# Latent attention taken in two groups of 256 queries, with the first pair's projection and routing in the second group's stream

## The chip, the cores and the metric

The kernel runs on one core of a Trainium2 chip. The metric is the device time of one execution in microseconds; the median over executions is compared. TensorE is PE, VectorE is DVE, ScalarE is ACT, GpSimd is POOL, and SP issues most of the loads.

## What is computed

A backbone of two layers over 512 latent tokens and 256 context tokens, width 1024, all in float32. Layer 0 mixes with a state-space scan, layer 1 with latent attention of 8 heads. Each layer ends in an expert retrieval: a query per head picks 16 of 16384 experts, so every token has 128 experts with gates. Of layer 1 only the latent tokens are needed. The parts that the change touches:

```python
def mla_attend(q_nope, q_rope, k_nope, k_rope, v):
    scale = (MLA_NOPE + MLA_ROPE) ** -0.5
    s = (jnp.einsum('bqhd,bkhd->bhqk', q_nope, k_nope)
         + jnp.einsum('bqhr,bkr->bhqk', q_rope, k_rope))
    p = jax.nn.softmax(s.astype(jnp.float32) * scale, axis=-1).astype(v.dtype)
    return jnp.einsum('bhqk,bkhd->bqhd', p, v)
...
    o_l, o_c = mla_mixer(...)
    h_lat = layer_norm(ALPHA * h_lat + mod_l[2] * o_l, ln_g[i, 0], ln_b[i, 0])
    f_l = peer_channel(h_lat * (1.0 + mod_l[4]) + mod_l[3], peer_w_q[i], peer_keys[i], peer_u[i], peer_v[i])
...
    idx, gate = peer_route(t, w_q, keys)
        act = jax.nn.gelu(jnp.einsum('td,tkd->tk', hb, u_tab[ib]), approximate=False) * gb
        return jnp.einsum('tk,tkd->td', act, v_tab[ib])
```

## The kernel before

Tokens come in tiles of 128: 0 and 1 are context, 2 to 5 latent. In layer 1, tile 5 is *gathered* (its experts' rows of `peer_u` and `peer_v` are fetched one by one by POOL and reduced on DVE), and tiles 4, 2 and 3 are *dense*: PE multiplies them with all 128 blocks of 128 experts, and a matrix of gates, mostly zero, picks from the result.

`mla` first projects down to the latents `cqT` and `ckvT` and makes the values `v`. Then for each of 8 heads `project` makes the head's queries (`qps`, rotary `rp` and `rs` for two heads at once) and keys (`kp_mla`, all 768 tokens), each split into a high and a low part by ACT and DVE. `scores` takes 128 queries at a time (four steps of a head): five matmuls for each of two score tiles `sp_mla`, maximum, exponential, scaling. `values`, two steps later, transposes the weights (`tp_ps`) and, at the head's last step, multiplies with `v` (`op_mla`).

After attention `out_steps` multiplies with the output weights (`op`), and its `norm` makes the normalised rows `h`; `query_steps` transposes and modulates them (`mt_ps`, `mT`), splits them into `Hall` (the dense experts' operand), and makes routing queries (`qp`). Both take a pair of tiles: the first pair is (5, 4), the second (2, 3). Before, both pairs' steps stand in one list, woven by `E1` and `E2`. `route` then finds a tile's experts, nearly all on DVE (lines 946 to 1021: `top16` and one-hots `oh`). `gate_matrix` turns a dense tile's routing into gate matrices, 16 groups of 8 tokens a tile (`e` and `o`, then `g_ps`, then `stage` to memory). `ahead` takes 48 of the 128 blocks of the dense product with U early (`U` split into `Uh`, `Ul`; `s_ps`), and `gather` yields gathered rows. `dense_held` does the rest: `s_ps` for the other 80 blocks and `acc` for all.

`merge` interleaves such streams: each step yields a time, and the stream with the smallest sum goes next; `side` streams don't keep the loop alive. This writes the program order. A scheduler then sets each engine's queue, and each engine takes its queue in that order. Tiles come from pools with a fixed number of buffers (20 of 4 KB per partition, 8 of 2 KB, 5 of `row`, 8 banks of PSUM); an instruction that writes a tile waits until the buffer is free. A use of a gathered row keeps its place in the program order on DVE. `peer_memory` closes the memory of attention's weights and opens `Hall` in it.

Of the kernel before, what the change touches and what calls it, by code (L numbers as in the profile page):

```python
# [20 lines left out]
D = 1024  # L21
# [24 lines left out]
KU, LH, KL, GQ = 2, 4, 2, 4  # L46
GA = 3
# [60 lines left out]
class Net:  # L108
# [763 lines left out]
    def peer_setup(self, l, dense, gather):  # L872
        self.keysT = self.t4([128, 8, 128], "keysT")
        self.load(self.keysT, self.a["peer_keysT"][l])
        self.tiles, self.gathered = dense, gather
        self.h1 = {}
        self.qT, self.m, self.gat, self.routed = {}, {}, {}, {}
        self.gm = self.dram.tile([16, 128, len(dense), 4, 8, 32], F32, name=f"gm{l}")
# [6 lines left out]
    def query_steps(self, l, pair, H):  # L885
# [504 lines left out]
    def mla(self, dense, gather):  # L1390
# [76 lines left out]
        wukv = W[:, 6144:10240].rearrange("p (k n) -> p k n", k=2)  # L1467
        cosT, sinT = W[:, 10240:10752], W[:, 10752:11264]
# [3 lines left out]
        for k in range(2):  # L1472
            self.load(wukv[:, k, :], a["mla_w_ukv"][k * 128:(k + 1) * 128, :])
# [3 lines left out]
        wv = wukv.rearrange("p k (h x d) -> p k h x d", h=8, x=2)  # L1477
        for ti in range(6):
            for hf in range(2):
                vp = self.ps([128, 4, 128], "vp")  # L1480
                for k in range(2):
                    PE.matmul(out=vp, lhsT=ckvT[k][:, ti * 128:(ti + 1) * 128], rhs=wv[:, k, hf * 4:(hf + 1) * 4, 1, :],
                              start=(k == 0), stop=(k == 1))
                S.copy(out=v[ti][:, hf * 512:(hf + 1) * 512].rearrange("p (h d) -> p h d", h=4), in_=vp)
        oT, heads = [], {}

        def project(h):
            if h % 2 == 0:
                oT.append(self.t4([128, 2, T_LAT], "oT"))
                rp, rs = self.ps([128, 512], "rp"), self.ps([128, 512], "rs")  # L1490
                for k in range(3):
                    PE.matmul(out=rp, lhsT=wuq[:, k, 1024 + h * 64:1024 + (h + 2) * 64], rhs=cqT[k], start=(k == 0), stop=(k == 2))
                for k in range(3):
                    PE.matmul(out=rs, lhsT=wuqs[:, k, h * 64:(h + 2) * 64], rhs=cqT[k], start=(k == 0), stop=(k == 2))
                qr, qt = self.t2([128, T_LAT], "qr"), self.t2([128, T_LAT], "qt")
                V.tensor_tensor(out=qr, in0=rp, in1=cosT, op=ALU.mult)
                V.tensor_tensor(out=qt, in0=rs, in1=sinT, op=ALU.mult)
# [169 lines left out]
```

## Time and profile before

| | |
|---|---|
| median of 2 executions | 4099.25 us (4098.07 to 4100.43) |
| profiled execution | 4107.66 us |
| its span in the trace | 4105.9 us |
| PE, DVE, ACT, POOL busy | 91%, 75%, 35%, 30% of the span |
| attention of layer 1 | 2466 to 2687 us |
| output and query projections | 2687 to 2788 us |
| four routes | 2788 to 2990 us |
| gate matrices, then the dense stage | 2990 to 3207 us, 3207 to 4090 us |

The profile is of one execution, and its stretches add up to its own time, which is 8.4 us above the median. The rows give for each engine how long it was busy in a stretch, for an instruction its start and duration, and in brackets how long its engine sat idle before it and what ended that. The limits of the stretches are the starts of the first instruction of the next kind of work.

### The profile page before, as it was taken

What the parts mean: (1) busy time and instruction counts of PE and PEld (TensorE: products, weight loads), DVE (VectorE), ACT (ScalarE), POOL (GpSimd) and SP (SyncE); (2) the same over time, 40 slices, a digit from 0 to 9 for tenths busy, and PEclk for the clock granted to TensorE, in tenths of its full rate; (3) what the DMA queues carried; (4) which work ended last, traced back from release to release, by engine and by line L of the source; (5) the groups of instructions that cost most, each with busy time, mean ns of one, the idle gap of its engine ahead of it and who ended that gap; (6) DMA issues with size and microseconds to landing.
All of it is one profiled execution on the core that took longest, in us unless ns stands there. A gap on an engine that the chain in (4) does not pass through costs nothing.

```text
span 4105.9 us, 52738 instructions
## 1 busy us (share of the span) xinstructions
PE 3719.0 (91%) x18955; PEld 3031.4 (74%) x18955; DVE 3068.7 (75%) x6143; ACT 1450.2 (35%) x2527; POOL 1238.6 (30%) x940
## 2 busy tenths in 40 slices
PE   6759999888689999999999989998887899999998
PEld 3537768677667878778888855568887788888887
DVE  9784387976867788888898844438977677777764
ACT  1321123366632232232332243323466333333332
POOL 5743000022412455556555300000011344444410
PEclk7879999899999999999999999999999999999999
DMA  5457234377888899999999820144477889888873
GB/s 182 134 176 247 80 131 152 96 241 249 293 311 290 291 338 352 337 354 330 342 338 346 301 98 3 44 169 140 123 234 247 317 327 334 318 320 321 328 271 102
DMA packets 380007, 986.06 MB, mean 240 GB/s; under 512 B 64992, under 2 KB 145376, under 8 KB 375136
## 3 DMA queue, kind: packets, MB, share of 16 engines
q1 hardware_dynamic: 198688, 501.34, 35.4%
q0 software_dynamic: 110592, 402.70, 27.4%
q10 hardware_dynamic: 70464, 78.65, 5.5%
q8 instruction: 149, 2.44, 0.2%
q14 instruction: 114, 0.93, 0.1%
HBM read 892.28 MB, written 90.21 MB: 239 GB/s over the span
## 4 chain that ended last, share of the span: by engine, by line
PE 57%; DVE 14%; issue 12%; DMA 7%; POOL 6%; ACT 3%; SPq 0%; POOLq 0%; ACTq 0%; DVEq 0%
PE s_ps L1111 20%; PE acc L1180 8%; PE acc L1255 8%; POOL row L1323 5%; PE qp L920 3%; PE op L791 3%; DMA U<-in_peer_uT 3%; DMA row<-in_peer_v,idx 2%; PE g_ps L1076 2%; PE zp L762 2%; DVE Ul L306 1%; PE op_mla L1560 1%; DVE w L645 1%; PE yp L697 1%; DMA row<-in_peer_u,idx 1%
## 5 line engine op out<-in xcount | busy, mean ns | idle before, releaser
L1111 PE MATMUL s_ps<-Hs,Uh 128*128 128x512 f32 (+1 forms) x4096 | 1187.4, 371 | 13.5 <-ACT Uh L305 13.5
L1323 POOL DMA_INDIRECT row<-in_peer_u,idx x384 | 528.8, 1377 | 2025.2 <-DVE row L1330 1148.2
L1111 PEld LDWEIGHTS s_ps<-Hs,Uh 128*128 128x128 f32 x4096 | 763.1, 190 | 116.2 <-ACT Uh L305 18.7
L1111 PE MATMUL s_ps<-Hs,Ul 128*128 128x512 f32 (+1 forms) x2048 | 759.6, 371 | 27.2 <-DVE Ul L306 27.1
L1255 PE MATMUL acc<-Ws,A 128*128 128x512 f32 x2976 | 689.1, 393 | 37.5 <-ACT A L305 21.4
L1255 PEld LDWEIGHTS acc<-Ws,A 128*128 128x128 f32 x2976 | 564.3, 190 | 160.6 <-ACT A L305 21.9
L1323 POOL DMA_INDIRECT row<-in_peer_v,idx x384 | 502.9, 1310 | 516.8 <-DVE f L1335 460.7
L306 DVE TENSOR_TENSOR Ul<-U,Uh 128x1024 fp32r<-128x1024 f32 x256 | 312.0, 1219 | 281.8 <-ACT Uh L305 273.6
L1335 DVE SCALAR_TENSOR_TENSOR f<-row,act,f 128x1024 f32<-128x1024 f32 x381 | 487.1, 1278 | 33.8 <-DMA row<-in_peer_v,idx 32.2
L1330 DVE SCALAR_TENSOR_TENSOR row<-row,m 128x1024 f32<-128x1024 f32 x384 | 461.0, 1218 | 42.7 <-DMA row<-in_peer_u,idx 41.7
L1111 PEld LDWEIGHTS s_ps<-Hs,Ul 128*128 128x128 f32 x2048 | 389.5, 190 | 82.3 <-DVE Ul L306 35.3
L305 ACT CAST Uh<-U 128x1024 fp32r<-128x1024 f32 x256 | 268.0, 1050 | 500.0 <-DMA U<-in_peer_uT 454.4
L1180 PE MATMUL acc<-Wh,A 128*128 128x512 f32 x1536 | 426.6, 391 | 12.2 <-ACT A L305 12.2
L1076 PE MATMUL g_ps<-o,o 128*128 128x128 f32 x1792 | 240.3, 293 | 114.5 <-ACT o L1059 72.1
L1180 PEld LDWEIGHTS acc<-Wh,A 128*128 128x128 f32 x1536 | 288.3, 188 | 66.7 <-ACT A L305 12.6
L1114 ACT ACTIVATE ge<-s_ps 128x512 f32<-128x512 f32 (+1 forms) x256 | 138.8, 543 | 556.4 <-PE s_ps L1111 551.1
L1076 PEld LDWEIGHTS g_ps<-o,o 128*128 128x128 f32 x1792 | 229.7, 206 | 126.2 <-ACT o L1059 124.5
L305 ACT CAST A<-ge 128x512 fp32r<-128x512 f32 (+1 forms) x256 | 144.6, 565 | 309.0 <-DVE ge L1236 227.1
L305 ACT CAST Ws<-W 128x512 fp32r<-128x512 f32 x256 | 152.1, 619 | 264.3 <-DMA W<-in_peer_v 217.7
L1180 PE MATMUL acc<-Wl,A 128*128 128x512 f32 x768 | 237.5, 390 | 0.0
L306 DVE TENSOR_TENSOR Ws<-W,Ws 128x512 fp32r<-128x512 f32 x256 | 174.3, 684 | 56.0 <-ACT Ws L305 55.7
L306 DVE TENSOR_TENSOR A<-ge,A 128x512 fp32r<-128x512 f32 (+1 forms) x256 | 158.5, 620 | 54.2 <-ACT A L305 53.7
(340 smaller groups left out, 4780.3 us busy)
## 6 DMA issues: line engine op xcount, KB each, us to landing
U<-in_peer_uT SPq DMA_DIRECT2D x256, 512.0 KB
W<-in_peer_v SPq DMA_DIRECT2D x256, 256.0 KB
W<-in_peer_v SPq DMA_DIRECT2D x128, 512.0 KB
gm<-stage ACTq DMA_DIRECT2D x28, 2048.0 KB
ada_wt<-in_ada_w SPq DMA_DIRECT2D x96, 512.0 KB
Gt<-gm SPq DMA_DIRECT2D x16, 2048.0 KB
Gt<-gm SPq DMA_DIRECT2D x16, 1536.0 KB
wq<-in_peer_w_q SPq DMA_DIRECT2D x40, 512.0 KB
```

Source lines behind the costliest of these rows:

```text
L305: self.nc.scalar.copy(out=hi, in_=x)
L306: lo_eng.tensor_tensor(out=lo, in0=x, in1=hi.bitcast(F32), op=ALU.subtract)
L791: nc.tensor.matmul(out=op, lhsT=y(i, k), rhs=W, start=(k == 0), stop=(k == KD - 1))
L920: PE.matmul(out=st["p"][:, h % 2, i * 128:(i + 1) * 128], lhsT=W[:, k, :], rhs=st[i][:, k, :], start=(k == 0), stop=(k == KD - 1))
L1076: PE.matmul(out=gp[:, t, :], lhsT=o[1][:, t4 * 4 + t, :], rhs=o[0][:, t4 * 4 + t, :], start=True, stop=True)
L1111: PE.matmul(out=sp, lhsT=x[:, k, :], rhs=self.Hs[:, y, k, :], start=(n == 0), stop=(n == 3 * KD - 1))
L1114: S.activation(out=ge, in_=sp, func=AF.Gelu)
L1180: PE.matmul(out=acc[d][hf], lhsT=A[b][:, x, c], rhs=Ws[y][:, hf * 512:(hf + 1) * 512], start=(b == 0 and n == 0), stop=(b == NB - 1 and n ...
L1255: PE.matmul(out=acc[hf][d], lhsT=A[b][:, x, c], rhs=Ws[:, y], start=(j == 0 and n == 0), stop=(j == SB - 1 and n == 2))
L1323: GP.indirect_dma_start(out=r, out_offset=None, in_=tab, in_offset=bass.IndirectOffsetOnAxis(ap=ik[:, k:k + 1], axis=0), element_offset=l ...
L1330: x = V.scalar_tensor_tensor(out=r, in0=r, scalar=1.0, in1=m, op0=ALU.mult, op1=ALU.mult, accum_out=act[:, k:k + 1])
L1335: x = V.scalar_tensor_tensor(out=f, in0=r, scalar=act[:, k:k + 1], in1=f, op0=ALU.mult, op1=ALU.add)
```

## The change

Attention runs over two groups of 256 queries, (tiles 4 and 5) and then (2 and 3), each over all heads; `project` is called for a pair and a head, one head ahead, and makes the keys of the head anew for each group. Keys and queries of a head stand in `kq`, half of a two-head buffer; the weights for values are loaded apart. While the second group is attended, the first pair's output projection, normalisation, queries and two routes stand in a side stream, and so does the gather. Only afterwards is `Hall` opened; the first pair's split into it is held back till then (`late`). The second pair's projection follows alone, beside the early blocks of U (which need all four tiles' queries), the gates (now begun when two tiles' queries are there) and the gather.

```diff
+TQ = 7.0
...
+    def query_steps(self, l, pair, H, late=False):
...
             if ti in self.tiles:
-                c = slice(i * 128, (i + 1) * 128)
-                H_ = H()
-                self.split(H_[:, 0, :, c], H_[:, 1, :, c], mT, nc.vector)
+                def parts():
+                    c = slice(i * 128, (i + 1) * 128)
+                    H_ = H()
+                    self.split(H_[:, 0, :, c], H_[:, 1, :, c], mT, nc.vector)
+
+                if late:
+                    self.late.append(parts)
+                else:
+                    parts()
...
-        W = self.big([128, 12288], "mla_w")
+        W = self.big([128, 9216], "mla_w")
...
+        wv = [self.t4([128, 8, 128], "wv") for _ in range(2)]
+        for k in range(2):
+            src = a["mla_w_ukv"][k * 128:(k + 1) * 128, :].rearrange("p (h x d) -> p h x d", h=8, x=2)
+            self.load(wv[k], src[:, :, 1, :])
+            self.load(wk[:, k], src[:, :, 0, :])
...
+        oT, heads = {}, {}
+
+        kq, pTs = self.t16([128, 2, 2 * T + 512], "kq", F32R), self.t16([128, 2, 6, 256], "pT")
+
+        def project(pair, h):
+
+            q0 = (min(pair) - 2) * 128
+            tq = slice(q0, q0 + 256)
+            if h % 4 == 0:
+                oT.setdefault(pair, []).append(self.t4([128, 4, 256], "oT"))
...
+                rp = self.ps([128, 2, 256], "rp")
+                for x, w in ((0, wuq[:, :, 1024 + h * 64:1024 + (h + 2) * 64]), (1, wuqs[:, :, h * 64:(h + 2) * 64])):
+                    for k in range(3):
+                        PE.matmul(out=rp[:, x], lhsT=w[:, k], rhs=cqT[k][:, tq], start=(k == 0), stop=(k == 2))
...
+            qnT = kq[:, h % 2, 2 * T:].rearrange("p (x q) -> p x q", x=2)
...
+                PE.matmul(out=qps, lhsT=wuq[:, k, h * 128:(h + 1) * 128], rhs=cqT[k][:, tq], start=(k == 0), stop=(k == 2))
...
+                    PE.matmul(out=kp[:, 0:n], lhsT=wk[:, k, h, :], rhs=ckvT[k][:, c0:c0 + n], start=(k == 0), stop=(k == 1))
+                self.split(kn[:, 0, c0:c0 + n], kn[:, 1, c0:c0 + n], kp[:, 0:n], V)
+            heads[pair, h] = qnT, qs, kn, pTs[:, h % 2]
...
+        def scores(pair, h, qi):
+
+            if h == qi == 0:
+                project(pair, 0)
+            qnT, qr, kn, _ = heads[pair, h]
...
+            if qi == 0 and h < 7:
+                project(pair, h + 1)
             return pe
 
-        def values(h, qi, pe):
-            pT = heads[h][3]
+        def values(pair, h, qi, pe):
+            pT = heads[pair, h][3]
             self.transpose_to(pT[:, :, qi * 128:(qi + 1) * 128], pe, 6)
-            if qi == 3:
-                op = self.ps([128, 512], "op_mla")
+            if qi:
+                op = self.ps([128, 256], "op_mla")
                 for k in range(6):
                     PE.matmul(out=op, lhsT=v[k][:, h * 128:(h + 1) * 128], rhs=pT[:, k, :], start=(k == 0), stop=(k == 5))
-                V.tensor_copy(out=oT[h // 2][:, h % 2, :], in_=op)
-            return 8.0
-
-        drain(pipeline([(lambda h=h, qi=qi: scores(h, qi), lambda pe, h=h, qi=qi: values(h, qi, pe))
-                        for h in range(8) for qi in range(4)], 2))
+                V.tensor_copy(out=oT[pair][h // 4][:, h % 4, :], in_=op)
+            return TQ
+
+        def attend(pair):
+            return pipeline([(lambda h=h, qi=qi: scores(pair, h, qi), lambda pe, h=h, qi=qi: values(pair, h, qi, pe))
+                             for h in range(8) for qi in range(2)], 2)
+
+        def rows(tile):
+            return [self.row_bc(self.mods, 14 * D, "m2", tile=tile), self.row_bc(a["ln_g"], 2 * D, "lng", tile=tile),
+                    self.row_bc(a["ln_b"], 2 * D, "lnb", tile=tile)]
+
+        def out(pair):
+            def y(i, k):
+                c = (pair[i] - min(pair)) * 128
+                return oT[pair][k // 4][:, k % 4, c:c + 128]
+
+            return self.out_steps(1, pair, a["mla_w_o"], y, lambda ti: self.hd[ti], lambda: self.rows2)
+
+        order = gather + dense
+        p, q = tuple(order[:2]), tuple(order[2:])
+        drain(attend(p))
         self.peer_setup(1, dense, gather)
-        self.peer_memory(1)
-        r = [self.row_bc(self.mods, 14 * D, "m2", tile=self.spare), self.row_bc(a["ln_g"], 2 * D, "lng", tile=self.spare),
-             self.row_bc(a["ln_b"], 2 * D, "lnb", tile=self.spare)]
-        order = gather + dense
-
-        def out(pair):
-            return self.out_steps(1, pair, a["mla_w_o"],
-                                  lambda i, k: oT[k // 2][:, k % 2, (pair[i] - 2) * 128:(pair[i] - 1) * 128], 
-                                  lambda ti: self.hd[ti], lambda: r)
-
-        p, q = tuple(order[:2]), tuple(order[2:])
-        (m0, q0), (m1, q1) = (self.query_steps(1, p, lambda: self.Hall[:, :, :, 0:256]),
+        self.rows2 = rows(lambda shape, name: self.pool.tile(shape, F32, tag="rows", bufs=3, name=name))
+        (m0, q0), (m1, q1) = (self.query_steps(1, p, lambda: self.Hall[:, :, :, 0:256], late=True),
                               self.query_steps(1, q, lambda: self.Hall[:, :, :, 256:512]))
-        o1 = out(q)
-        steps = out(p) + o1[:E1] + m0 + o1[E1:] + q0[:E2] + m1 + q0[E2:] + q1
-
         self.gathering = self.gather(1, R1)
+        first = chain(pipeline(out(p) + m0 + q0, LT), *(self.route(ti) for ti in p))
+        merge(attend(q), side=(first, self.gathering))
+        while len(self.qT) < 2:
+            next(first)
+
+        def memory(_):
+            self.peer_memory(1)
+            for f in self.late:
+                f()
+            self.rows2 = rows(self.spare)
+            return 0.0
+
+        steps = [(lambda: None, memory)] + out(q) + m1 + q1
         self.aheads = self.ahead(1, [b for b in range(128) if b % 8 < A1], 4)
-        self.gates = self.gate_matrices(4)
-        merge(scaled(pipeline(steps, LT), FA), chain(*(self.route(ti) for ti in order)), side=(self.aheads, scaled(self.gates, FG1)))
+        self.gates = self.gate_matrices(2)
+        merge(scaled(pipeline(steps, LT), FA), chain(first, *(self.route(ti) for ti in q)),
+              side=(self.aheads, scaled(self.gates, FG1), self.gathering))
```

What the scheduler made of it is seen at three places. The first is on PE, where the first pair's output projection (`op`) ends and the normalised rows are transposed (`mt_ps`). Before:

```order
L1560 MATMUL op_mla<-pT,v 128x512 x6
L791 MATMUL op<-wo,oT 128x512 x52
L296 MATMUL mt_ps<-ident,h 128x128 x8
L791 MATMUL op<-wo,oT 128x512
L904 MATMUL m_ps<-ident,mT 128x128 x4
L791 MATMUL op<-wo,oT 128x512
L904 MATMUL m_ps<-ident,mT 128x128 x4
L296 MATMUL mt_ps<-ident,h 128x128 x8
```

and in the changed kernel, where `sp_mla` are scores of the second group:

```order
L1531 MATMUL kp_mla<-ckvT,mla_w 128x512 x2
L1531 MATMUL kp_mla<-ckvT,mla_w 128x256 x2
L287 MATMUL tp_ps<-ident,pe 128x128 x6
L792 MATMUL op<-wo,oT 128x512 x10
L297 MATMUL mt_ps<-ident,h 128x128 x8
L912 MATMUL m_ps<-ident,mT 128x128 x5
L1548 MATMUL sp_mla<-kq 128x512
```

The 32 matmuls of the first pair were followed by 20 of the second pair; now the transposes stand right behind the last of the 32, and the next scores behind them.

The second place is on DVE, in attention. `mx`, `nm`, `rsm` and `pe` are a step's maximum, its negative, its reciprocal sum and its weights. Before:

```order
L1542 TENSOR_TENSOR nm<-mx 128x1
L1543 TENSOR_SCALAR nm<-nm 128x1
L1539 TENSOR_REDUCE mx<-sp_mla 128x1
L1549 TENSOR_TENSOR rsm<-smx 128x1
L1539 TENSOR_REDUCE mx<-sp_mla 128x1
L1550 RECIPROCAL rsm<-rsm 128x1
L1542 TENSOR_TENSOR nm<-mx 128x1
L1551 TENSOR_SCALAR pe<-pe,rsm 128x768
L1543 TENSOR_SCALAR nm<-nm 128x1
L1549 TENSOR_TENSOR rsm<-smx 128x1
L1550 RECIPROCAL rsm<-rsm 128x1
```

and in the last third of the second group now, where `rw`, `scr` and `tk_tmp` are routing's and `row` a gathered expert:

```order
L1556 TENSOR_TENSOR nm<-mx 128x1
L954 MAX rw_20778<-scr 128x8
L1557 TENSOR_SCALAR nm<-nm 128x1
L954 MAX rw_20778<-scr 128x8
L955 MAX_INDEX rw_20778<-rw_20778,scr 128x8
L1338 SCALAR_TENSOR_TENSOR row,act<-row,m 128x1024
L956 MATCH_REPLACE tk_tmp<-rw_20778,scr 128x128 x2
L957 MAX rw_20778<-tk_tmp 128x8 x2
L958 MAX_INDEX rw_20778<-rw_20778,tk_tmp 128x8 x2
L1563 TENSOR_TENSOR rsm<-smx 128x1
```

Routing's instructions and gathered rows stand between the links of one softmax. Of both routes only the second tile's one-hots come behind the last of attention.

The third place is on DVE where the gates (`e`, `o`) end. `Ul` is an early block's low part. Before, ahead of the dense stage's first `Wl`:

```order
L1330 SCALAR_TENSOR_TENSOR row,act<-row,m 128x1024
L1054 TENSOR_TENSOR e<-iota_68,iT 128x2048
L1062 TENSOR_TENSOR o_24260<-e,gT 128x768
L1330 SCALAR_TENSOR_TENSOR row,act<-row,m 128x1024 x3
L306 TENSOR_TENSOR Ul<-U,Uh 128x1024
L1330 SCALAR_TENSOR_TENSOR row,act<-row,m 128x1024 x4
L306 TENSOR_TENSOR Wl<-W,Wh 128x1024
```

and now, where the last two rows go on in turn for 13 blocks (`row` sometimes more than once):

```order
L1070 TENSOR_TENSOR o_24194<-e,gT 128x768
L1062 TENSOR_TENSOR e<-iota_68,iT 128x2048
L1070 TENSOR_TENSOR o_24215<-e,gT 128x768
L1338 SCALAR_TENSOR_TENSOR row,act<-row,m 128x1024
L307 TENSOR_TENSOR Ul<-U,Uh 128x1024
```

Fewer early blocks stand among the gates, and 13 remain behind them, where before 3 did on PE. Before the dense stage 90 gathered rows are used, 32 before the change.

## Rows read from the trace of the kernel before

**Rows 1.** The page, totals: busy us (share of the span) and instructions.
```profile
PE 3719.0 (91%) x18955; PEld 3031.4 (74%) x18955; DVE 3068.7 (75%) x6143; ACT 1450.2 (35%) x2527; POOL 1238.6 (30%) x940
```

**Rows 2.** Busy time in stretches of the second layer: us, then each engine (instructions).
```profile
core 0: us, PE busy (x) PEld busy (x) DVE busy (x) ACT busy (x) POOL busy (x), PEclk, DMA share, GB/s
2466.00:2687.00 221.00, 212.46 (x771) 119.89 (x770) 102.51 (x276) 84.61 (x227) 0.00 (x0) 0.98 0.10 36
2687.00:2788.00 101.00, 100.98 (x553) 69.64 (x551) 41.10 (x124) 24.96 (x57) 0.00 (x0) 1.00 0.49 162
2788.00:2990.00 202.00, 171.78 (x1053) 163.72 (x1053) 191.75 (x876) 87.48 (x136) 4.70 (x5) 0.93 0.42 134
2990.00:3184.00 194.00, 159.71 (x1070) 157.44 (x1071) 137.64 (x154) 132.04 (x239) 37.48 (x28) 0.94 0.74 246
...
3207.00:4090.00 883.00, 868.58 (x4224) 769.82 (x4224) 645.37 (x812) 304.14 (x421) 312.76 (x219) 1.00 0.82 295
```

**Rows 3.** PE in order of time, one head of attention: start, us, line, operation.
```profile
2556.90 5.42 PE L1560 MATMUL op_mla<-pT,v 128*128 128x512 f32 x12 [0.46 <-ACT pT L287]
...
2565.21 0.48 PE L1534 MATMUL sp_mla<-knT,qnT 128*128 128x512 f32 x1
...
2567.72 0.87 PE L286 MATMUL tp_ps<-ident,pe 128*128 128x128 f32 x6
2568.43 2.74 PE L1492 MATMUL rp<-cqT,mla_w 128*128 128x512 f32 x6
...
2573.58 2.74 PE L1510 MATMUL qps<-cqT,mla_w 128*128 128x512 f32 x6
2576.16 2.74 PE L1516 MATMUL kp_mla<-ckvT,mla_w 128*128 128x512 f32 x8
2578.71 1.03 PE L1534 MATMUL sp_mla<-knT,qnT 128*128 128x512 f32 x2
```

**Rows 4.** Chain that ended last, in order of time: start, us, step.
```profile
2686.64 44.63 PE op L791 x104
...
2744.55 17.86 PE qp L920 x160
...
3214.14 4.21 PE s_ps L1111 x24
```

**Rows 5.** DVE, PE and ACT in order of time, first pair's normalisation, modulation.
```profile
2713.29 0.69 DVE L797 TENSOR_TENSOR res<-op,m 128x512 f32<-128x512 f32 x1 [12.18 <-PE op L791]
...
2724.70 2.35 DVE L268 TENSOR_TENSOR h<-h,lnb 128x1024 f32<-128x1024 f32 x2
...
2731.11 1.04 PE L296 MATMUL mt_ps<-ident,h 128*128 128x128 f32 x8
...
2762.89 3.25 ACT L299 ACTIVATE mT<-mt_ps,modT 128x128 f32<-128x128 f32 x9 [3.37 <-PE mt_ps L296]
```

**Rows 6.** Routing: DVE busy for tiles `Ul`, then `e`, then one-hot lines.
```profile
2788.00:2990.00 202.00, 33.37 (x28) 0.93 0.42 134
...
2788.00:2990.00 202.00, 19.24 (x18) 0.93 0.42 134
...
L1020 DVE TENSOR_TENSOR oh<-oh 128x1024 bf16<-128x1024 bf16 (+2 forms) x24 | 10.0, 460 | 0.1
...
L1018 DVE TENSOR_TENSOR oh<-oh,sib 128x2048 bf16<-128x2048 bf16 x8 | 9.6, 1216 | 0.0
...
L1015 DVE TENSOR_TENSOR oh<-iota,ab 128x2048 bf16<-128x2048 bf16 x8 | 9.5, 1212 | 0.0
```

**Rows 7.** DVE groups by form, 2440 to 4090: gathered rows times `m`.
```profile
L1330 DVE SCALAR_TENSOR_TENSOR row<-row,m 128x1024 f32<-128x1024 f32 x128 | 153.8, 1217 | 0.0
```

**Rows 8.** Chain links of gathered rows, layer one; who waited for line 1323.
```profile
1259.99 6.13 DMA row<-in_peer_u,idx
...
  DVE row L1330: 41.7, 32
```

**Rows 9.** What PE waited for, 2806 to 3207: us, times, longest.
```profile
PE g_ps L1076 <- ACT o L1059: 28.1, 10, 6.5
```

**Rows 10.** Busy time in a stretch of routing, with the granted clock.
```profile
2850.00:2900.00 50.00, 38.11 (x213) 35.89 (x212) 47.12 (x192) 24.37 (x41) 0.00 (x0) 0.83 0.21 66
```

More of the change, by code (lines that the diff above doesn't have):

```diff
@@ L877, in peer_setup @@
         self.qT, self.m, self.gat, self.routed = {}, {}, {}, {}
+        self.late = []
         self.gm = self.dram.tile([16, 128, len(dense), 4, 8, 32], F32, name=f"gm{l}")
@@ L883, in peer_memory @@
         self.Hs = self.Hall[:, :, :, T_LAT - len(self.tiles) * 128:]
-    def query_steps(self, l, pair, H):
+    def query_steps(self, l, pair, H, late=False):
         nc = self.nc
@@ L1481, in mla @@
                 for k in range(2):
-                    PE.matmul(out=vp, lhsT=ckvT[k][:, ti * 128:(ti + 1) * 128], rhs=wv[:, k, hf * 4:(hf + 1) * 4, 1, :],
+                    PE.matmul(out=vp, lhsT=ckvT[k][:, ti * 128:(ti + 1) * 128], rhs=wv[k][:, hf * 4:(hf + 1) * 4, :],
                               start=(k == 0), stop=(k == 1))
                 S.copy(out=v[ti][:, hf * 512:(hf + 1) * 512].rearrange("p (h d) -> p h d", h=4), in_=vp)
-        oT, heads = [], {}
-        def project(h):
-            if h % 2 == 0:
[L1489 to L1497, printed above, removed]
-                V.tensor_tensor(out=qr, in0=qr, in1=qt, op=ALU.add)
-                qs = self.row([128, 2, T_LAT], "qs", F32R)
@@ L1501, in project @@
                 for x in range(2):
                     r, o = slice(64 * x, 64 * x + 64), slice(64 - 64 * x, 128 - 64 * x)
-                    S.copy(out=qs[r, x], in_=qr[r])
-                    V.tensor_tensor(out=qs[o, x], in0=qr[r], in1=qs[r, x].bitcast(F32), op=ALU.subtract)
-            else:
-                qs = heads[h - 1][1]
-            qnT = self.row([128, 2, T_LAT], "qnT", F32R)
-            qps = self.ps([128, 512], "qps")
+                    S.copy(out=qs[r, x], in_=qr[r, 0])
@@ L1509, in project @@
+                    V.tensor_tensor(out=qs[o, x], in0=qr[r, 0], in1=qs[r, x].bitcast(F32), op=ALU.subtract)
+            else:
+                qs = heads[pair, h - 1][1]
+            qnT = kq[:, h % 2, 2 * T:].rearrange("p (x q) -> p x q", x=2)
+            qps = self.ps([128, 256], "qps")
             for k in range(3):
-                PE.matmul(out=qps, lhsT=wuq[:, k, h * 128:(h + 1) * 128], rhs=cqT[k], start=(k == 0), stop=(k == 2))
+                PE.matmul(out=qps, lhsT=wuq[:, k, h * 128:(h + 1) * 128], rhs=cqT[k][:, tq], start=(k == 0), stop=(k == 2))
@@ L1511, in project @@
             self.split(qnT[:, 0], qnT[:, 1], qps, V)
-            kn = [self.t4([128, T], "knT", F32R) for _ in range(2)]
+            kn = kq[:, h % 2, 0:2 * T].rearrange("p (x t) -> p x t", x=2)
             for c0, n in ((0, 512), (512, 256)):
@@ L1515, in project @@
                 for k in range(2):
-                    PE.matmul(out=kp[:, 0:n], lhsT=wukv[:, k, h * 256:h * 256 + 128], rhs=ckvT[k][:, c0:c0 + n],
-                              start=(k == 0), stop=(k == 1))
-                self.split(kn[0][:, c0:c0 + n], kn[1][:, c0:c0 + n], kp[:, 0:n], V)
-            heads[h] = qnT, qs, kn, self.t16([128, 6, T_LAT], "pT")
-        def scores(h, qi):
-            if qi == 0:
-                project(h)
-            qnT, qr, kn, _ = heads[h]
+                    PE.matmul(out=kp[:, 0:n], lhsT=wk[:, k, h, :], rhs=ckvT[k][:, c0:c0 + n], start=(k == 0), stop=(k == 1))
[5 more added lines that the diff above has]
+            qnT, qr, kn, _ = heads[pair, h]
             x = h % 2
```

18 lines of the change are left out of this document (10 added, 8 removed).

## Prediction

> **What bounds the kernel now.** I read the page's totals first, then a table of stretches, then single rows. Over the whole span TensorE (PE) is busy 91% and VectorE (DVE) 75% [rows 1], but that is a mean over stages with different limits. The table of stretches [rows 2] cuts the second layer where the work changes. Attention, 2466 to 2687 us, keeps PE busy 212 of 221 us and DVE 103. Output projections and query projections, 2687 to 2788, keep PE busy throughout. Routing, 2788 to 2990, is DVE's: 192 of 202 us, with PE at 172. Gate matrices, 2990 to 3184, fill no engine (PE 160, DVE 138, ACT 132 of 194). After 23 us of tail the dense stage runs 883 us with PE busy 869. So the change can only move the 741 us from 2466 to 3207, and at most 14 us of PE's idle time behind them. In the four stretches before the tail PE is idle for 73 us, 64 of them in routing and gates; with the tail that is all there is to win, less what is added.
>
> **What the change adds and moves.** I take the new program in the order of its instructions and price each stretch by rows. Counts are from the order; all times are from the trace of before.
>
> *First group's attention.* In the rows of one head [rows 3], a step of scores and transposes takes 3.22 us (2565.21 to 2568.43). The value product takes 5.42 us for 512 queries and its wait 0.46. The two rotary projections take 5.15 us per pair of heads, the query projection 2.58, and the key projection 2.55 (2576.16 to 2578.71). At four steps, a head costs 26.4 us; eight are 211, and the stretch took 221, so the ramps at both ends are 10. With 256 queries a head costs two steps 6.44, value product and wait 3.16, rotary 1.29, query 1.29, but the key projection whole again: 2.55. That is 14.7; eight heads are 118, with 7 of ramp **125 us**. Both groups pay 236 where before paid 211: 8 x 2.55 = 20 us of doubled key projection, the rest repeated waits.
>
> *Second group up to its first routing matmul.* PE's order holds 3 rotary (7.7 us), 6 query (7.7) and 6 key projections (15.3), 9 score steps at 2.51 (22.6), 7 groups of transposes at 0.71 (5.0), 3 value products (9.5), 24 transposes at 0.11 (2.6), the first pair's output projection at 44.63 us per 104 passes, two passes to a matmul (64 passes, 27.5), and its queries at 17.86 per 160 (256 passes, 28.6) [rows 4]. Sum 126.5. To that comes a wait which before did not have. The first pair's output projection is now followed at once by the transposes of the normalised rows, with the next scores queued behind them on PE. Before, 20 more output matmuls stood there, and PE went on through them. In the trace the normalisation runs from 2713.29 to the first finished tile at 2725.88 (half of the 2.35 us of two) [rows 5], 12.6 us, now bare (before, the transposes stand at 2731.11, PE at work till then). The modulation behind it costs 0.36 us a block on ACT (9 in 3.25 us), 8 blocks for each of two tiles: 5.8. With 5 of ramp: **150 us**. Bounds 138 (normalisation covered after all) and 165.
>
> *Rest of the second group's attention.* From here DVE's queue holds two routings between the attention's small steps. A route costs (191.75 - 33.37 - 19.24) / 4 = 34.8 us of DVE: the routing stretch, less its 28 differences of U and 9 pairs of one-hots, over four tiles [rows 2, 6]. The one-hot tail of the second (29.1 / 4 = 7.3 us, lines 1015 to 1020) comes later, so 62.3. Seven attention steps at 102.51 / 32 = 3.2, and 0.2 for the doubled key splits, are 23.8. Eight gathered rows at 1.217 are 9.7 [rows 7]. Sum 95.8; in the routing stretch DVE was 95% busy [rows 2], so **100 us**. PE has some 51 us of work here (7 score steps, 9 transposes, 5 value products, one pair's projections, 32 routing matmuls). So 49 of the 100 us are PE idle with no filler: the blocks of U that filled routing before need the memory that opens only after attention. This is where "routing under attention" loses: only PE's 51 us are free cover for two routes.
>
> *The second pair's own chain.* Its projection, normalisation and queries now run alone; before, each pair's waits lay under the other's matmuls. The end of the first dense tile's route (13 us of DVE), its first gate group (5), 22 of 32 output matmuls behind that (18.9), 3 gate groups of matmuls (2.7), normalisation 12.6 with 3 gathered rows queued among its steps (3.7), modulation 2.9, transposes 1.8, queries 28.6 and two gate groups (1.8), scores to DVE (2): **94 us**. Bounds 80 and 105.
>
> *The other two routes.* 69.6 us of routing, 17 differences at 33.37 / 28 = 1.19 (20.3), 5 one-hot pairs at 19.24 / 9 = 2.14 (10.7), 19 gathered rows (23.1): 123.7, at 95% **130 us**, with PE's 72 us of U blocks below it.
>
> *Gates and the blocks left.* 35 of 48 groups remain here; before, 39 remained and took 194 us [rows 2]: **174 us**. The lower bound is PE's own work: 35 groups of 16 passes at 0.111 and 18 blocks at 4.21 [rows 4], 138. Then 13 blocks of U stand alone where before had 3: 13 x 4.21 = **55 us**, which covers the 23 us tail.
>
> *The gather* is begun earlier: 90 rows are used before the dense stage instead of 32. Each costs DVE 1.2 us. In the dense stage that was free (DVE 645 of 883 us [rows 2]); 46 of the rows now stand in stretches that DVE or a bare chain sets, and these are in the sums. What it gives back is at most the dense stage's 14 us of PE idle time; I take 5. The landing time of a row in an idle stretch is not shown in before. The nearest row is a link of the chain in the first layer at 6.13 us, and DVE waited for rows of this kind 32 times for 41.7 us in all [rows 8], 1.3 us each; I take nothing more, since rows are fetched ahead. The Trainium skill ("DMA: Bandwidth & Descriptors", Anatomy of one DMA) gives about 2 us plus bytes over 436 GB/s for such a transfer, an estimate of 3.2 us for a 512 KB row; by it a bare first row would add 3 us to the sum. No row here shows it.
>
> **Sum.** 125 + 150 + 100 + 94 + 130 + 174 + 55 = 828 against 741: +87, less 5: +82. On the profiled execution's 4107.66 us that is 4190; on the median, which lies 8.4 lower, **4181 us** (+2.0%). A measurement of this kernel tells about 2%, some 82 us, from no change, so the forecast sits on that edge.
>
> **Rivals.**
> *It stays within no change: the relieved DVE pays back.* In routing and gates PE waited 28.1 us for one-hots from ACT [rows 9]. If the gate stretch ran at PE's own pace, 138 instead of 174, and the dense stage lost all its 14 us, the total is 82 - 36 - 9 = +37: 4136. It decides if the wait per gate group falls below some 0.1 us. For it: more groups are made ahead. Against: each group costs ACT and DVE what it did.
> *The gather's rows hold up the attention.* DVE works in order, and each use of a row stands ahead of a reduction that scores wait for. If each of the 8 rows in the tail arrives 6.13 us late [rows 8], +49: 4230. For it: two of the five row buffers' users (keys' rotary part, queries' rotary part) are still held there. Against: 3 us or more of other work stand between uses. That the gather doesn't start under attention at all is excluded by the order.
> *The clock falls.* With PE busy 38 of 50 us the granted clock was 0.83 [rows 10], so a third of that time at 1.2 GHz. PE's 54 us on the second pair's bare chain at that share would add 18, and the same on the first pair's bare output and query matmuls 18: 4217. The Trainium skill ("TensorE: Matmul & The Clock Gate", Part 1) says that the low clock is the default and activity lifts it; by that, idle PE is charged twice. The rows so far show it only partly.
> *Faster.* It would take 82 us off, while PE's idle time in the four stretches is 73 and 20 are added: nearly excluded.
>
> **Chances.** Forecast 0.52 (4155 to 4210, so half of it beyond 2%), pay-back 0.23, late rows 0.12, clock 0.10, faster 0.03. Slower by over 2%: 0.26 + 0.12 + 0.10 = 0.48; within 2%: 0.26 + 0.23 = 0.49; faster 0.03. The ends of all terms at once give about 4090 and 4280; leaving out 2 in 10 the range is 4120 to 4240.
>
> **What would show it.** Attention's first group near 125 us. A PE wait of about 12 us for `h` ahead of `mt_ps` while scores stand behind. DVE over 90% busy and PE near half in the last 100 us of attention. Dense stage starting some 80 us later, with the gather's last row earlier in it. I am wrong if the second group's tail runs at PE's pace, or if PE shows little idle time between attention and gates.

## The result and the profile after

The changed kernel took 4218.03 us (median of 2 runs) where before took 4099.25: ratio 1.029, 95% interval 1.0246 to 1.0334, slower by over 2%. Timed again beside the experiments it took 4208.98 (4 runs): 1.0267, interval 1.0249 to 1.0285. That is what I expected (4205 to 4212) if the first two runs were longer ones. The forecast was 4181, its range 4120 to 4240. The direction and the place of the loss were right, the sum of the stretches was, by the traces, some 24 us short (852 us for 828).

The part before attention differs between profiled executions also where the kernel is the same: the first rotary matmul of the second layer starts anywhere from 2453.6 to 2471.8 us, in two profiles of the changed kernel at 2471.8 and 2462.7. So besides the medians I compare one distance in each trace, from that matmul to the first matmul of the dense stage. It is 741.5 us before (2465.9 to 3207.4), 851.8 after (2471.8 to 3323.6), 848.0 in the second profile of after. The rest, dense stage and end, takes 898.5, 895.4 and 894.7. Nearly the whole loss lies in that distance.

The page's totals of the changed kernel, beside [rows 1]: 45 us more of busy time on PE, 11 more on DVE.

```profile
PE 3763.7 (89%) x19211; PEld 3099.7 (73%) x19211; DVE 3080.1 (73%) x6195; ACT 1459.0 (35%) x2557; POOL 1229.1 (29%) x940
```

The table of stretches of the changed kernel, cut at the prediction's steps, answers to [rows 2]: us, then busy time of each engine (instructions), the granted clock, DMA. In order: first group; second group up to the first routing matmul; rest of its attention; the second pair's chain; the other two routes; gates; the blocks left; dense stage. The last line is all seven stretches ahead of the dense stage.

```profile
core 0: us, PE busy (x) PEld busy (x) DVE busy (x) ACT busy (x) POOL busy (x), PEclk, DMA share, GB/s
2471.40:2590.90 119.50, 115.59 (x514) 83.88 (x513) 59.14 (x163) 47.69 (x130) 0.00 (x0) 1.00 0.06 21
2590.90:2732.40 141.50, 128.94 (x634) 92.92 (x633) 50.39 (x128) 41.04 (x105) 0.00 (x0) 0.95 0.19 62
2732.40:2829.00 96.60, 63.64 (x290) 46.14 (x290) 92.89 (x502) 25.68 (x66) 13.13 (x13) 0.82 0.30 94
2829.00:2931.00 102.00, 78.64 (x421) 60.00 (x421) 64.89 (x114) 33.31 (x68) 24.43 (x18) 0.85 0.71 241
2931.00:3066.50 135.50, 105.53 (x600) 100.80 (x600) 126.16 (x511) 53.37 (x82) 22.55 (x20) 0.87 0.60 188
3066.50:3252.50 186.00, 152.73 (x999) 150.87 (x1000) 126.45 (x143) 119.71 (x217) 35.97 (x26) 0.90 0.72 240
3252.50:3323.60 71.10, 58.49 (x312) 56.69 (x311) 38.17 (x53) 21.71 (x30) 23.11 (x19) 0.93 0.89 319
3323.60:4206.00 882.40, 867.30 (x4224) 771.09 (x4224) 584.01 (x703) 304.37 (x422) 228.71 (x162) 1.00 0.72 261
2471.40:3323.60 852.20, 703.56 (x3763) 591.30 (x3761) 558.09 (x1610) 342.51 (x696) 119.19 (x95) 0.91 0.49 162
```

PE's idle time in the distance is 852.2 - 703.6 = 149 us. Before it was 73 in the four stretches and 12 in the tail. Read line by line: attention without routes (the first two lines) leaves PE idle 4 and 12.6 us; from the first route on PE idles 33, 23, 30, 33 and 13 us and the granted clock is 0.82 to 0.93.

The 12.6 is nearly all one wait. PE in order of time at the first pair's transposes, the place that [rows 5] priced at 12.6 us bare:

```profile
2648.15 8.75 PE L792 MATMUL op<-wo,oT 128*128 128x512 f32 x20
2668.85 1.94 PE L297 MATMUL mt_ps<-ident,h 128*128 128x128 f32 x8 [11.95 <-DVE h L269]
...
2672.01 0.77 PE L1548 MATMUL sp_mla<-kq 128*128 128x512 f32 x1
```

The scores at 2672.01 need nothing of the normalisation; they stand behind it in PE's order. In the tail of attention DVE sets the pace: it is busy 92.9 of 96.6 us, PE 63.6. First what PE waited for from 2732 to 2829 us (us, times, longest), then the last 39 us of that stretch as a window:

```profile
PE tp_ps L287 <- DVE pe L1565: 24.7, 3, 12.2
2790.00:2829.00 39.00, 13.76 (x45) 10.48 (x45) 39.00 (x212) 5.04 (x14) 10.32 (x10) 0.65 0.45 141
```

In this window DVE has no idle time at all, and the softmax's last multiplication `pe`, which PE's transposes need, queues behind top-k and one-hots of the routes. The granted clock is 0.65 there, so more than half of that time at 1.2 GHz.

The chain that ended last in the changed kernel, its links that are transfers. Between attention and dense stage before's chain had only one pair of these, at its very end (the gates' store, 15.87 us, and a load behind it, 6.73):

```profile
2785.15 4.77 DMA row<-in_peer_u,idx
...
2890.43 3.35 DMA wq<-in_peer_w_q
...
2911.49 8.53 DMA wq<-in_peer_w_q
...
3253.14 8.90 DMA gm<-stage
3262.49 9.27 DMA U<-in_peer_uT
```

Where the 90 early rows were used: DVE's instructions of the row's line alone, by stretch from the tail on. A row is two instructions, so 8, 19, 19, 26 and 18 rows.

```profile
2732.40:2829.00 96.60, 9.69 (x16) 0.82 0.30 94
2829.00:2931.00 102.00, 22.73 (x38) 0.85 0.71 241
2931.00:3066.50 135.50, 23.13 (x38) 0.87 0.60 188
3066.50:3252.50 186.00, 31.86 (x52) 0.90 0.72 240
3252.50:3323.60 71.10, 21.59 (x36) 0.93 0.89 319
```

### The profile page after: what moved, and what is told of

It is laid out like the page before. It is cut to its first block, busy times and chain, and to the rows that moved or that the text cites. A ratio compares the mean times of both kernels' runs of the same rounds, so it can differ in the third digit from the quotient of the medians.

```text
span 4219.0 us, 53368 instructions
## 1 busy us (share of the span) xinstructions
PE 3763.7 (89%) x19211; PEld 3099.7 (73%) x19211; DVE 3080.1 (73%) x6195; ACT 1459.0 (35%) x2557; POOL 1229.1 (29%) x940
## 4 chain that ended last, share of the span: by engine, by line
PE 55%; DVE 16%; issue 15%; POOL 6%; DMA 5%; ACT 2%; SPq 1%; POOLq 0%; DVEq 0%; ACTq 0%
PE s_ps L1119 18%; PE acc L1188 10%; PE acc L1263 6%; POOL row L1331 6%; PE qp L928 3%; PE op L792 3%; PE g_ps L1084 2%; PE zp L763 2%; DMA row<-in_peer_v,idx 2%; DMA U<-in_peer_uT 2%; DVE Ul L307 1%; DVE rw L958 1%; DVE tk_tmp L956 1%; DVE w L646 1%; DVE row L1338 1%
## 5 line engine op out<-in xcount | busy, mean ns | idle before, releaser
L1331 POOL DMA_INDIRECT row<-in_peer_u,idx x384 | 520.3, 1355 | 1949.7 <-DVE row L1338 984.3
```

Source lines behind the costliest of these rows:

```text
L1331: GP.indirect_dma_start(out=r, out_offset=None, in_=tab, in_offset=bass.IndirectOffsetOnAxis(ap=ik[:, k:k + 1], axis=0), element_offset=l ...
```

## The experiments

My theory was the prediction's: the split costs the doubled keys; routes under attention and the bare chain cost the most; early rows cost their DVE time. The rivals: the split itself is the dear part; the routes or rows fill holes and are free; the low clock is what costs. The table gives each kernel's median, the 95% interval of its ratio to before, and the distance from the first rotary matmul to the dense stage in its trace.

| kernel | median us | 95% interval of the ratio | distance us |
|---|---|---|---|
| before | 4099.25 | | 741.5 |
| changed | 4218.03 | 1.0246 to 1.0334 | 851.8 |
| changed, again | 4208.98 | 1.0249 to 1.0285 | 848.0 |
| two groups alone | 4119.27 | 1.0030 to 1.0064 | 758.1 |
| two groups, second's keys left out | 4101.63 | 0.9999 to 1.0018 | 737.2 |
| routes after attention | 4170.04 | 1.0157 to 1.0190 | 810.8 |
| gather late | 4161.08 | 1.0132 to 1.0166 | 807.4 |
| normalisation covered | 4186.88 | 1.0200 to 1.0234 | 837.6 |
| routes after, gather late | 4144.77 | 1.0095 to 1.0130 | 784.0 |
| the same, normalisation covered | 4129.42 | 1.0049 to 1.0085 | 767.2 |
| first 46 rows light | 4180.52 | 1.0169 to 1.0209 | 818.4 |
| gates from the other queue | 4204.41 | 1.0233 to 1.0267 | 844.3 |
| added matmuls in the tail | 4208.37 | 1.0233 to 1.0277 | 848.2 |

**Two groups alone.** Both groups are attended first; all behind it stands as before.

```diff
         drain(attend(p))
+        drain(attend(q))
...
+        steps = out(p) + o1[:E1] + m0 + o1[E1:] + q0[:E2] + m1 + q0[E2:] + q1
...
-        merge(attend(q), side=(first, self.gathering))
...
-        self.gates = self.gate_matrices(2)
...
+        self.gates = self.gate_matrices(4)
...
```

> Attention in two groups of 256 queries, and nothing else: after both groups the output projections, queries, routes, gates and gather follow as in the kernel before. Theory (the sum of the prediction: the split costs the doubled key projection and little more; the moves cost the rest): the first group took 119.5 us in the changed kernel, so two take 239 against 221, +18; the changed kernel also came to its attention 5.4 us later, which this kernel keeps if the new layout of the weights is the reason: 4117 to 4123 us, ratio 1.004 to 1.006. Rival (the split itself, with its shared key buffers and half-wide matmuls, is what is dear, and the moves gain nothing and lose nothing): near 4218.

Measured 4119.27, as the theory said. The window of the whole distance shows more: it holds the same PE instructions as the changed kernel's last line above (3764 and 3763), busy 28 us less, at a clock of 0.96 against 0.91.

```profile
2467.70:3226.20 758.50, 675.60 (x3764) 570.27 (x3762) 498.76 (x1494) 343.75 (x698) 47.99 (x37) 0.96 0.43 142
```

So against the split alone the changed kernel loses 94 us: 28 in which PE is busy longer with the same instructions and 66 in which it stands idle (23 and 67 in the second profile of the changed kernel, where PE was busy 698.1 us).

**The keys left out**, on top of the two groups:

```diff
-            for c0, n in ((0, 512), (512, 256)):
+            for c0, n in ((0, 512), (512, 256)) if pair == p else ():
                 kp = self.ps([128, 512], "kp_mla")
```

> Two groups of attention and nothing else moved, and the second group leaves out its key projection and the split of the keys: it reads what the first group's last two heads left in the key buffers. What the output holds is not the reference. Theory (the split's price is the eight key projections of 2.55 us done twice): 20 us less than the 4119 of two groups, 4096 to 4104, no different from before. Rival (repeated ramps and half-wide matmuls are the price, the keys are hidden): 4112 to 4122.

Measured 4101.63, no different from before; against two groups alone the distance shrank by 20.9 us and the median by 17.6, for eight projections priced at 20.4. The split costs its doubled keys, with their splits on ACT and DVE, and nothing else that shows.

**Routes after attention.** The first pair's routes leave the side stream.

```diff
-        first = chain(pipeline(out(p) + m0 + q0, LT), *(self.route(ti) for ti in p))
-        merge(attend(q), side=(first, self.gathering))
+        first = pipeline(out(p) + m0 + q0, LT)
+        merge(attend(q), side=(first,))
...
-        merge(scaled(pipeline(steps, LT), FA), chain(first, *(self.route(ti) for ti in q)),
+        merge(scaled(pipeline(steps, LT), FA), chain(first, *(self.route(ti) for ti in order)),
```

> The changed kernel, but under the second group's attention only the first pair's output projection and queries; its two routes come after attention, beside the second pair's output projection and queries. Theory (routes under attention are the loss: DVE sets the last 97 us of attention with PE busy 64, and then the second pair's chain of 103 us has no routes to lie under): the tail of attention falls to about 55, the chain to about 90, while 4 gate groups move to later stretches (+8 to +14): 45 us less than the changed kernel, 4160 to 4185. Rival (routes under attention are cover won, the loss lies in the split and in the gather): two routes of 35 us of DVE come out from under attention, of which PE's 33 idle us come back: 4225 to 4255.

Measured 4170.04: the theory. In windows of this kernel the tail of attention is now PE's (48 of 50 us) at full clock, and the second pair's output and queries take 84.5 us with the routes under them. That is 64 us less than the changed kernel's tail and chain. The next two lines take 23 of it back: the four routes (196.7 us, where two took 135.5), then the gates and the blocks left (218.7 for 257.1).

```profile
2723.50:2773.80 50.30, 47.91 (x225) 35.59 (x224) 23.75 (x67) 20.48 (x57) 0.00 (x0) 1.00 0.27 89
2773.80:2858.30 84.50, 65.52 (x400) 48.23 (x398) 71.64 (x358) 20.56 (x41) 8.49 (x8) 0.90 0.41 136
2858.30:3055.00 196.70, 142.90 (x819) 134.50 (x819) 184.28 (x682) 79.57 (x126) 37.63 (x30) 0.88 0.61 194
3055.00:3273.70 218.70, 180.77 (x1175) 176.44 (x1175) 146.06 (x169) 136.71 (x242) 46.42 (x33) 0.94 0.78 265
```

What is late next is the second pair's own normalisation, now mixed with the routes on DVE. PE's wait for it in the window of 84.5 us:

```profile
PE mt_ps L297 <- DVE h L269: 17.5, 1, 17.5
```

**Gather late.** The gather leaves both side streams and begins beside the gates.

```diff
-        merge(attend(q), side=(first, self.gathering))
+        merge(attend(q), side=(first,))
...
-              side=(self.aheads, scaled(self.gates, FG1), self.gathering))
+              side=(self.aheads, scaled(self.gates, FG1)))
```

> The changed kernel, but the gather is taken up only where the kernel before takes it up, beside the gates: no row is fetched or used under attention, in the second pair's chain or beside the other two routes. Theory (each row costs its 1.2 us of DVE where DVE or a bare chain sets the pace, and its buffer keeps the query weights waiting): 8 rows less in the tail of attention (-10) and the chain's first row (-5), the 6 us that PE waited for wq (-6), 19 rows beside the routes (-23, of which PE's own pace may keep half): 4175 to 4190. Rival (the rows fill holes of DVE, the early start is free): 4213 to 4223. Second rival (the early start pays in the dense stage): over 4225.

Measured 4161.08: the theory's direction, and some 14 us below its best end. Most of that is the first timing, 4218, from which it was reckoned: the distance fell by 44.4 us, and the theory's terms add up to 44 at most. By windows of this kernel the tail took 87.7 us (96.6 with rows), the second pair's chain 87.1 (102.0), routes and gates together 301.8 (321.5). The chain is where I had counted too little, 6 us where 15 came back; the tail gave 9 of the 15 expected:

```profile
2726.60:2814.30 87.70, 64.46 (x293) 46.33 (x293) 85.78 (x499) 26.01 (x67) 0.00 (x0) 0.84 0.15 49
2814.30:2901.40 87.10, 73.19 (x418) 55.91 (x416) 41.22 (x63) 32.82 (x66) 3.75 (x4) 0.88 0.49 163
2901.40:3203.20 301.80, 250.12 (x1598) 243.82 (x1598) 229.62 (x610) 173.32 (x299) 32.08 (x25) 0.94 0.60 195
```

The dense stage and the end took 893.8 us here and 895.4 with 48 more rows taken off it. Over the six traces with the gather early (routes after attention not counted) that part averages 893.7 us (886.5 to 902.0), over the six with it late 897.6 (893.8 to 903.1): some 4 us bought, no more than its scatter, for 44 paid.

**First 46 rows light.** The changed kernel's fetches, without their work on DVE.

```diff
-                    if ph == 0:
+                    if l and ph == 0 and k < 46:
+                        x = V.tensor_copy(out=act[:, k:k + 1], in_=r[:, 0:1])
+                    elif ph == 0:
```

> The changed kernel, but of the gathered tile's first 46 rows in the second layer only the first element is copied (128x1) in place of the product and sum over 1024: the dot products of these rows are left out, and the output is not the reference. The rows are fetched as early as in the changed kernel, into the same buffers. Theory (a row costs its DVE time, 1.15 us each where DVE or a bare chain sets the pace): most of what the late gather gave back, less the waits for wq, which share the buffers: 4170 to 4185. Rival (the price is the transfers and the buffers): 4203 to 4221.

Measured 4180.52: the theory. Of the 44 us of distance that the late gather gave back, the rows' DVE work alone gives back 33 (851.8 to 818.4); in the medians of the changed kernel's second timing it is 28 of 48. The 46 small copies still take DVE 0.15 us each. PE's wait for `wq` in the second pair's chain stays at 4.4 us, as below (6.2 in the changed kernel, none with the gather late), so fetching has a price of its own: the query weights are loaded into the same five row buffers.

```profile
PE qp L928 <- DMA wq<-in_peer_w_q: 4.4, 2, 2.4
```

**Normalisation covered.** Two steps of attention are let past ahead of the transposes.

```diff
-        first = chain(pipeline(out(p) + m0 + q0, LT), *(self.route(ti) for ti in p))
+        first = chain(pipeline(out(p) + [(lambda: None, lambda _: 9.0)] + m0 + q0, LT), *(self.route(ti) for ti in p))
```

> The changed kernel, but two steps of the second group's attention are put between the first pair's output projection and the transposes of its normalised rows, so that PE has 16 us of work during the normalisation (it waited 11.95 us there). Theory (the tail of attention is DVE's, so that attention steps drawn forward are worth there only their DVE time, 3.4 us each): the bare wait is gone, the routes start about 4 us later, the tail is 7 us shorter: 4211 to 4218. Rival (a bare wait of PE counts in full): 4206.

Measured 4186.88, by the median better than both said. The distance fell by 14.2 us against the first profile and 10.4 against the second, which is what the rival said (12). The median gained more; in this trace dense stage and end also took the shortest of all, 886.5 us, for which I see no cause in the edit. The wait is gone, and in windows of this kernel the routes start after 135.2 us (141.5), the tail takes 85.2 (96.6), and the second pair's chain gives some back (108.0 against 102.0; PE waits 22.5 us there for the end of a route, `rt`, against 6.5):

```profile
2576.80:2712.00 135.20, 133.00 (x663) 96.08 (x661) 51.78 (x136) 42.57 (x110) 0.00 (x0) 1.00 0.21 65
2712.00:2797.20 85.20, 62.28 (x273) 43.30 (x272) 81.82 (x428) 23.52 (x60) 10.44 (x11) 0.80 0.30 93
2797.20:2905.20 108.00, 71.68 (x407) 56.68 (x407) 71.07 (x173) 33.26 (x67) 21.33 (x18) 0.79 0.66 224
```

My theory erred in adding two whole steps to the first window: only 4 us of PE work came in there (133.0 against 128.9) against 12 us of wait. Both gains add, the earlier routes and the DVE work taken out of the tail.

**Both undone, and then covered too.** The first has the edits of routes after and gather late together, the second adds the covered normalisation.

> The changed kernel with both undone: the first pair's routes come after attention, and the gather is taken up only beside the gates. Theory (a gathered row costs its 1.15 us of DVE wherever DVE sets the pace): with the routes after attention alone, 30 rows were used beside the four routes, where DVE was busy 184 of 197 us, so 25 to 35 us less than that run's 4170: 4133 to 4147, still slower than before by the split (20) and by the bare normalisation. Rival (routes and rows fill the same holes of PE, the two gains are one): 4155 to 4165.

> Routes after attention, gather late, and two attention steps put ahead of the first pair's transposes: the three together. What is left of the change is the split, and the first pair's output projection and queries under the second group's attention. Theory (with the routes gone PE sets the whole of attention, so that the covered wait counts once and in full, 12 us): 12 less than the 4145 without the cover: 4128 to 4138. Rival (the cover paid before only through the routes that came sooner): 4141 to 4149. Neither reaches the 4119 of the split alone, since the second pair's normalisation stays bare.

Measured 4144.77 and 4129.42: the theory both times. Without routes in the tail the cover is worth 15 us (16.8 of distance). In this last kernel PE's waits from 2582 to 2770 us, the first two lines, name no normalisation any more, the longest is 0.9 us. The second pair's stays bare (third line, 2770 to 2900 us), where two groups alone show no such wait:

```profile
PE op_mla L1576 <- ACT pT L288: 2.9, 6, 0.6
PE m_ps L912 <- ACT mT L300: 1.1, 2, 0.9
PE mt_ps L297 <- DVE h L269: 17.5, 1, 17.5
```

**Gates from the other queue.**

```diff
-            self.load(Gt[sb], self.gm[sb])
+            (nc.gpsimd if l and sb < 2 else nc.sync).dma_start(out=Gt[sb], in_=self.gm[sb])
```

The reason for it is SP's queue in the changed kernel, in order of time: the two `Gt` loads need the last gates stored (3253.14 + 8.90 = 3262.04), and one load of U stands between them, nine behind.

```profile
3231.07 10.16 SPq L167 DMA_DIRECT2D U<-in_peer_uT  x3
3262.06 0.33 SPq L167 DMA_DIRECT2D Gt<-gm  x1
3262.49 0.39 SPq L167 DMA_DIRECT2D U<-in_peer_uT  x1
3262.98 0.40 SPq L167 DMA_DIRECT2D Gt<-gm  x1
3263.43 28.48 SPq L167 DMA_DIRECT2D U<-in_peer_uT  x9
```

> The changed kernel, but the second layer's first two loads of gates are issued from POOL's queue in place of SP's. In the changed kernel they stand among the loads of U on SP and wait there until the last gates are stored (8.9 us), and PE starves for U. Theory (the tail's idle time is that queue's, not the blocks'): the 71 us of the last 13 blocks fall by about 10: 4205 to 4211. Rival (the loads are at the rate of the DMA engines, 319 GB/s there, and the wait only moves): 4214 to 4224.

The time, 4204.41, cannot be told from the 4208.98 of the changed kernel in its second timing. In the trace the last blocks took 67.0 us instead of 71.1, not 61. PE's waits in the changed kernel and in this one:

```profile
PE s_ps L1119 <- ACT Uh L306: 9.2, 2, 7.7
```

```profile
PE s_ps L1119 <- DVE Ul L307: 6.2, 2, 4.7
PE acc L1188 <- ACT A L306: 2.5, 1, 2.5
```

PE's idle time there is 8.7 us for 12.6. So the queue is part of it and most of the wait only moves; whether to the rate of the transfers (324 GB/s there) I have not shown.

**Added matmuls in the tail**, against the clock as the cause:

```diff
+            if pair == q and h > 3:
+                warm = self.ps([128, 256], "warm")
+                for n in range(8):
+                    PE.matmul(out=warm, lhsT=v[0][:, 0:128], rhs=ckvT[0][:, 0:256], start=True, stop=True)
+                S.copy(out=self.sm([128, 1], "wk"), in_=warm[:, 0:1])
             self.transpose_to(pT[:, :, qi * 128:(qi + 1) * 128], pe, 6)
```

The last added line copies one column of the result on ACT; nothing reads the copy.

> The changed kernel with added work: in heads 4 to 7 of the second group, 8 matmuls of 128x256 on data that lies there (two passes each, 3.4 us at full clock) stand on PE ahead of each step's transposes, 8 times, where PE waited for DVE. Their result is used by nothing. Theory (the clock is part of the loss: the same instructions kept PE busy 704 us in the changed kernel and 676 us with two groups alone, at a mean clock of 0.91 against 0.96): the tail's clock rises from 0.82 to above 0.95, the work in the tail and the output projection behind it run at full rate: 0 to 10 us less, 4208 to 4218, although 27 us of work are added. Rival (PE's time there is not slack, the clock not worth it): 10 to 27 us more, 4228 to 4245.

Measured 4208.37, at the theory's edge; beside the second timing of the changed kernel it is no change, and the distances are 848.2 and 848.0. The tail's window says why: the clock rose to 0.95 and PE was busy 24 us longer, and the stretch took 97.1 us in place of 96.6.

```profile
2725.70:2822.80 97.10, 87.32 (x423) 67.66 (x422) 93.57 (x504) 26.93 (x75) 12.59 (x13) 0.95 0.30 93
```

The rival falls (PE's time there is slack), and of the theory the half that mattered falls too: in the tail the low clock costs nothing, since DVE sets its length.

## Why the prediction was right in direction and short in size

Undone one after the other, the medians make this account of the 110 us of the second timing: gather late 48 (4208.98 to 4161.08), routes after attention 16 (to 4144.77), cover of the normalisation 15 (to 4129.42), the rest of the reordering 10 (to 4119.27: the first pair's projections under attention, gates begun earlier, the second pair's normalisation left bare), split 20 (to before). The order matters: with the routes moved first, they are worth 39 and the late gather 25. A likely reason, not tested by itself, is the count of rows used ahead of the gates: 46 in the changed kernel, 33 with the routes after attention.

*First group*, 125 predicted, 119.5 measured; *up to the first route*, 150 and 141.5, with the bare wait at 11.95 for 12.6; *rest of attention*, 100 and 96.6, DVE at 96%. These three hold, each a few us high, and so do the doubled keys at 20 (20.9 by distance, 17.6 by medians). In the tail PE's 51 us of work took 63.6, at a granted clock of 0.82, so PE idled 33 us and not 49.

*The second pair's own chain*, 94 predicted, 102.0 measured. The step that failed is "3 gathered rows queued among its steps (3.7)": 19 rows were used in this stretch. The prediction knew of them: its "46" rows "are in the sums", but the sums charge 8, 3 and 19, which is 30. (The terms of this stretch also add up to 93, not 94.) Without rows it took 87.1, with light rows 92.6 (2821.4 to 2914.0 in that trace), so 9 us come from the rows' DVE work and 5 from the fetches and small copies, most of it PE's wait for `wq` (4.4). Nor did the rows stand in the normalisation: PE's wait for `h` is 10.1 or 10.2 us in all three kernels. They stood ahead of the end of a route, `rt`, for which PE waited 2.3 us in both other kernels. PE's waits in this stretch of the changed kernel:

```profile
PE mt_ps L297 <- DVE h L269: 10.2, 1, 10.2
PE tr_ps L1048 <- DVE rt L1029: 6.5, 2, 5.4
PE qp L928 <- DMA wq<-in_peer_w_q: 6.2, 2, 3.4
```

"I take nothing more, since rows are fetched ahead" was wrong for the buffers: beside DVE, the rows held up another user of their pool.

*The other two routes*, 130 and 135.5, DVE at 93%: near enough. *Gates*, 174 and 186. I scaled 194 us by 35 of 48 groups against 39, which shrinks the blocks of U as well. They did not shrink: 1070 PE instructions [rows 2] less 39 x 16 are 446 for the blocks, 999 less 35 x 16 are 439. Taking off the four groups' 64 passes at 0.111 alone gives 194 - 7 = 187. This is arithmetic on the rows; no run tested it.

*The blocks left*, 55 and 71.1. Here the step that failed is that the blocks cover the tail. Before, the tail of 23 us had PE busy 11.2, so 12 idle; after, with ten more blocks in hand, it is again 71.1 - 58.5 = 12.6 idle. In part that is because the blocks' own loads queue behind those of the gates, which wait for the gates' store: issuing the gates' loads from the other queue took back 4 of it. What the other 8.7 hang on is open. The other 3.5 of the 16 us are PE's: 58.5 busy for 55, at a clock of 0.93.

*The dense stage gives back 5*: by the averages above 4, within the scatter.

So the sum was nearer than its terms, and part of that is luck: three terms were 17 us high together and four 42 us low.

**The rivals.** *Pay-back* did not come: the gate stretch kept 33 us of PE idle time, for 34 before. *Rows hold up the attention* did not come either: the first row took 4.77 us from issue to use, but DVE waited for rows only once in the whole tail, 1.8 us:

```profile
DVE row L1338 <- DMA row<-in_peer_u,idx: 1.8, 1, 1.8
```

The Trainium skill's estimate ("DMA: Bandwidth & Descriptors", Anatomy of one DMA) of 3.2 us for that bare row is below the 4.77; the measurement decides, and as most of the rows' price was their DVE time, the difference matters little. *The clock falls* came as far as its rows: 28 us more of PE time for the same instructions than with two groups alone (23 in the second profile), where the rival had 36. Its own row gives less than it took: 54 us at a clock of 0.83 become 65, so 11 more and not 18. And the stretch up to the first route kept PE busy 128.9 us for the 126.5 priced, 2 more and not 18. That its 4217 lies beside the measured 4218 is chance. What share of it is on the path is open: in the tail none is, by the added matmuls; in the chain and the gates I changed it only together with other things (routes and gates at 0.94 without early rows, 0.89 with them).

## What to carry to other kernels

Before work of a second engine is put under a stage, count that engine's own small steps in the stage: here softmax needed DVE a little at every step, and some 62 us of routing (the prediction's estimate) ahead of them in one queue turned a PE-bound tail into a DVE-bound one, while the matmuls that used to run beside routing could not come along, as their memory opened later. An early start of a background stream is worth what idle time its present place lacks; the gather had room in the dense stage, so nearly all that was paid to take rows forward was lost. And when a stretch is re-priced by scaling, scale each kind of work by its own count.

## What the runs showed of the hardware that I had not expected

Matmuls that fill PE's waits can be free: 24 us of them in a stretch of 97 raised the granted clock from 0.82 to 0.95 and changed no time. The Trainium skill ("TensorE: Matmul & The Clock Gate", Part 1) has activity lift the clock, and the trace agrees; that a lifted clock need not be time is what the run adds. A load that waits for a store holds up what stands behind it on its queue: SP issued its three loads of U by 3241.2, and the next instruction only at 3262.06, 0.02 us after the store of the gates had landed by the chain's links.
